# The first stage of an encoder kernel: c as one row, identity transposes ahead of the first product, and the second token half prepared in the gap at the loop's end

## The chip, the core and the metric

The kernel runs on one core of a Trainium2 chip. The core has a matrix engine (TensorE, PE in the rows), a vector engine (VectorE, DVE), an activation engine (ScalarE, ACT), a general engine (GpSimd, POOL) and SyncE (SP), which here issues all transfers between the chip's main memory and the on-chip memory. Each engine runs its own queue in order and waits on semaphores for what others produce. The metric is the device time of one execution, in microseconds (us); the median of the runs of the kernel before is 1440.84 us (three runs, 1440.55 to 1444.22).

## The reference

Two encoder layers over 1024 tokens of width 1024, one sequence, all in 32-bit floats. What matters here is how a layer begins:

```python
def _modulation(c, ada_w, ada_b):
    mod = jax.nn.silu(c) @ ada_w + ada_b
    shift, scale, gate = jnp.split(mod[:, None, :], 3, axis=-1)
    return shift, scale, gate

# layer i
shift, scale, gate = _modulation(c, ada_w[i], ada_b[i])
h = _rmsnorm(x, norm_g[i]) * (1.0 + scale) + shift
# layer 0 (differential attention)
proj = h @ w_in
q, k, v, z = jnp.split(proj, [DA_WIDTH, 2 * DA_WIDTH, 3 * DA_WIDTH], axis=-1)
q = _rope(q.reshape(b, s, 2 * DA_HEADS, DA_QK_DIM), positions)
```

So before any product of layer 0 there are the sums of squares of each token of x, the SiLU of c, and the products of c with 2048 columns of the modulation's weights (another 3072 columns are needed later).

## The kernel before, in words

**Precision.** Every product is made of three: both operands are split into a high part (rounded to the format that PE reads fast) and the rest, and high·high, high·rest and rest·high are added up in one accumulator (`mm3`, L181 to L183). A weight is split by a cast on ACT (L226, L544) and a subtraction on GpSimd or VectorE (L227, L545).

**The head.** c is loaded as a broadcast over all 128 partitions (L421, 512 KB), turned into 2·SiLU(c) by a tanh on ACT (L424) and one VectorE operation (L425), and copied into an accumulator bank of two bank widths (`cb`, L556), from which VectorE reads it. The four tiles of x's first token half (`xs0`, 128 tokens each) follow it in SP's queue. Their squares are summed on ACT (tiles 0 and 2, L531) and VectorE (tiles 1 and 3, L534); `inv_rms` (L463) and a power on GpSimd (L168) give the factors; ACT scales the first 256 columns (L564), VectorE the others (L618).

**The loop (first token half).** It runs over the 8 blocks `k` of 128 input features. For each, VectorE multiplies c with two tiles of modulation weights and sums (`mod_pair`: L431 twice, L439), which gives this block's shift and scale for each feature; PE turns four 128x128 pieces of x (`trh`, L485); ACT writes scale·x + shift as the high part `h0h` (L490) and in full as `h` (L492); GpSimd subtracts to get `h0l` (L495). One turn later PE adds the block into five accumulators: four of v (`vacc`, one for each 128 tokens, 512 columns; L635, L636 with `h0h`, L640 with `h0l`) and one of the K strip of head 0 (`kacc`, L637, L638, L641). Each turn needs two modulation tiles (`ada`, 512 KB each, 4 buffers), one tile of v's weights (`wvr`, 256 KB, 2 buffers) and half a tile of K weights.

**The gap.** After the loop stand: the squares of the second token half (`xs1`), the angles and sines of the rotary embedding (L572 to L591, with the table load that ACT needs for sines), the first half of head 0's q strip (`strip_half`, L181 to L183, 24 products of 128x512), the storing of the four v accumulators (`store_v`: cast L358, subtraction L359, transfer L361), the normalisation of `xs1` (L474).

**The second token half.** Eight blocks again: transposes (into `trh` and `trc` in turn), `h0h`, `h` and `h0l`, and 12 products a block, three blocks later. In between `mods_g` hands out the products of c for layer 1's modulation. Then come the K strip's second half, v's second 512 columns (`wv1`, accumulators `vps`), the q strip's second half, and the attention.

**What sets the order.** The program text is turned into one queue for each engine by a scheduler that goes by the order of the text and by when it expects an operand or a buffer to be ready. `tc.issue_after(i)` holds the instructions of its block behind `i` in their engine's queue; `tc.keep_in_program_order` keeps one where the text has it. A tile with a tag takes one of the `bufs` buffers of that tag in turn and waits until its last user is done.

## Time and profile before

| | |
|---|---|
| median of 3 runs | 1440.84 us |
| profiled execution | 1442.18 us, span of its instructions 1440.4 us |
| PE busy | 1390.9 us, 97% of the span |
| VectorE, ACT, GpSimd busy | 63%, 51%, 42% |
| mean granted clock of PE | 0.994 |
| first transpose of x on PE | at 14.35 us |
| longest wait of PE | 14.3 us, for the scaled x |
| DMA queue over the first 36 us | 325 GB/s |

A row of the timeline reads: start, duration, engine, line of the kernel, operation, what it writes and reads, shape, count, and in brackets how long the engine was idle just before it and for whom. PE's matmuls overlap, so the distance from one start to the next tells the pace, not the duration. The stretches (windows) give busy time and count of each engine between two moments, then the clock that the throttle granted to PE, the busy share of the transfer engines and their rate. A DMA's "us to landing" runs from its issue on SP until its data have arrived.

### The profile page before, as it was taken

How to read it: one execution, taken by the hardware profiler on the slowest of the kernel's cores; microseconds unless marked ns; L12 is line 12 of the kernel's file. 1: busy time of each engine (PE TensorE's matmuls, PEld its weight loads, DVE VectorE, ACT ScalarE, POOL GpSimd, SP SyncE). 2: the span in 40 equal slices, each digit the busy share in tenths (PEclk: the TensorE clock that was granted, in tenths of full speed). 3: DMA queues.
4: the chain of work that ended last, by engine and by line, in shares of the span. 5: the costliest groups of instructions: out<-in, count | busy, mean ns of one | idle time of the engine just before them, and what ended most of it. 6: DMA issues, size and time to landing. Idle time of an engine off the chain costs nothing. (4 is left out here: it accounts for less than half of the span.)

```text
span 1440.4 us, 20566 instructions
## 1 busy us (share of the span) xinstructions
PE 1390.9 (97%) x7388; PEld 1162.7 (81%) x7388; DVE 911.3 (63%) x1360; ACT 732.4 (51%) x1299; POOL 607.5 (42%) x483
## 2 busy tenths in 40 slices
PE   5999999999999999998999999989999999999997
PEld 4777788888888887887787787868888888888886
DVE  6657787667777767677445867254666555555355
ACT  5523366656565655566343643334554554545442
POOL 4316164656464646463561335313141331412562
PEclk9999999999999999999999999999999999999999
DMA  9777823333333333237653232566343433336663
GB/s 326 238 239 229 267 69 100 81 107 84 96 96 88 96 88 91 86 96 244 239 182 124 63 100 81 159 175 170 112 122 116 130 97 81 103 98 212 218 204 137
DMA packets 129766, 203.20 MB, mean 141 GB/s; under 512 B 18432, under 2 KB 55424, under 8 KB 129664
## 3 DMA queue, kind: packets, MB, share of 16 engines
q1 hardware_dynamic: 129664, 201.89, 46.4%
q8 instruction: 58, 0.95, 0.3%
q14 instruction: 44, 0.36, 0.1%
HBM read 132.68 MB, written 45.56 MB: 124 GB/s over the span
## 5 line engine op out<-in xcount | busy, mean ns | idle before, releaser
L381 ACT CAST pth<-tr 128x512 fp32r<-128x512 f32 x256 | 150.2, 587 | 277.3 <-PE tr L379 274.2
L396 DVE TENSOR_REDUCE nm<-s 128x1 f32<-128x1024 f32 x192 | 234.0, 1219 | 73.5 <-PE s L770 64.4
L382 DVE TENSOR_TENSOR ptl<-tr,pth 128x512 fp32r<-128x512 f32 x256 | 176.2, 688 | 137.5 <-ACT pth L381 136.8
L227 POOL TENSOR_TENSOR wl<-wraw,wh 128x512 fp32r<-128x512 f32 (+2 forms) x82 | 102.7, 1255 | 231.9 <-ACT wh L226 198.1
L398 ACT ACTIVATE e<-s,nm 128x1024 f32<-128x1024 f32 x128 | 143.5, 1121 | 30.4 <-DVE nm L396 29.9
L379 PE MATMUL tr<-ident,e 128*128 128x128 f32 x1024 | 154.9, 274 | 4.1 <-DVE ptl L382 3.7
L379 PEld LDWEIGHTS tr<-ident,e 128*128 128x128 f32 x1024 | 121.5, 141 | 45.2 <-DVE ptl L382 21.3
L181 PE MATMUL acc<-h0h,wh 128*128 128x512 f32 x360 | 150.1, 417 | 2.2 <-DVE v_hl L359 2.2
L181 PE MATMUL pv<-pth,vt 128*128 128x256 f32 x512 | 147.4, 288 | 0.0
L182 PE MATMUL pv<-ptl,vt 128*128 128x256 f32 x512 | 146.3, 286 | 0.0
L183 PE MATMUL pv<-pth,vt 128*128 128x256 f32 x512 | 144.8, 283 | 0.0
L183 PE MATMUL acc<-h0h,wl 128*128 128x512 f32 x360 | 142.3, 395 | 0.7 <-POOL wl L227 0.7
L182 PE MATMUL acc<-h0l,wh 128*128 128x512 f32 x360 | 141.6, 393 | 0.0
L1010 POOL TENSOR_TENSOR wol<-wor,woh 128x512 fp32r<-128x512 f32 x64 | 84.5, 1338 | 86.2 <-ACT woh L1009 81.1
L181 PEld LDWEIGHTS pv<-pth,vt 128*128 128x128 f32 x512 | 97.7, 191 | 3.1 <-ACT pth L381 0.4
L182 PEld LDWEIGHTS pv<-ptl,vt 128*128 128x128 f32 x512 | 97.8, 191 | 2.6
L183 PEld LDWEIGHTS pv<-pth,vt 128*128 128x128 f32 x512 | 97.9, 191 | 0.1
L328 POOL TENSOR_TENSOR rp_sw<-rp_sw,sinT 128x512 f32<-128x512 f32 x42 | 55.2, 1315 | 75.3 <-DMA rp_sw<-rp_raw 70.7
L770 PE MATMUL s<-ks,qa 128*128 128x512 f32 x256 | 82.2, 402 | 3.1 <-DVE e L778 2.7
L323 POOL TENSOR_TENSOR rp_r<-rp_raw,cosT 128x512 f32<-128x512 f32 x38 | 49.8, 1311 | 83.4 <-ACT rp_raw L318 52.3
L778 DVE SCALAR_TENSOR_TENSOR e<-s,z,e 128x1024 f32<-128x1024 f32 x64 | 82.1, 1283 | 2.1
L770 PE MATMUL s<-ks,qb 128*128 128x512 f32 x256 | 81.0, 395 | 0.0
(600 smaller groups left out, 3343.5 us busy)
## 6 DMA issues: line engine op xcount, KB each, us to landing
ada<-in_ada_ss SPq DMA_DIRECT2D x32, 512.0 KB, 6.1
wraw<-in_w_s SPq DMA_DIRECT2D x64, 256.0 KB, 2.9
vS<-v_hl SPq DMA_DIRECT2D x32, 512.0 KB, 5.2
vt<-vS SPq DMA_DIRECT2D x32, 512.0 KB, 4.0
wor<-in_w_out SPq DMA_DIRECT2D x64, 256.0 KB, 3.9
rp_sw<-rp_raw SPq DMA_DIRECT2D x168, 64.0 KB, 2.0
bc_s<-bc_d SPq DMA_DIRECT2D x34, 256.0 KB, 4.3
oS<-bc_s SPq DMA_DIRECT2D x30, 256.0 KB, 2.2
```

The costliest lines, as they stand in the source:

```text
L181: PE.matmul(psum, ah, bh, start=first, stop=False)
L182: PE.matmul(psum, ah, bl, start=False, stop=False)
L183: PE.matmul(psum, al, bh, start=False, stop=last)
L227: sub = (V if pair_of else G).tensor_sub(l_[:, :n], raw[:, :n], f32v(h_[:, :n]))
L379: PE.transpose(tr[:, j, :], p[:, kt * P : (kt + 1) * P], ident)
L381: mk["S"] = S.copy(pth[kh][:, :, dst], tr).ins
L382: mk["V"] = V.tensor_sub(ptl[kh][:, :, dst], tr, f32v(pth[kh][:, :, dst])).ins
L396: mk["V"] = V.reduce_max(nm, s_ps, axis=AX.X, negate=True).ins
L398: mk["S"] = S.activation(e, s_ps, AF.Exp, bias=nm, scale=1.0, accum_out=zs).ins
L770: PE.matmul(s_ps[:, kc * HF : (kc + 1) * HF], src[:, c, ql], KS[h][kc][:, c, :], start=fst, stop=not fst)
L778: combined.append(V.scalar_tensor_tensor(out=e0, in0=e1, scalar=z1[:, 0:1], in1=e0, op0=ALU.mult, op1=ALU.add).ins)
L1010: in_turn(G.tensor_sub(lo, raw, f32v(hi)))
```

## The change

- c is loaded as one row (4 KB). Its SiLU is computed on one partition and spread over the 128 partitions of `cb` by two products with a row of ones, full-precision 32-bit, 512 columns each. The copy that later modulations read is made from `cb` on ACT at block 2.
- PE gets 64 transposes of the identity ahead of the first transposes of x, the two products standing behind the seventeenth; 12 more stand between the first four transposes of x and the first product.
- The first token half's factors are computed for three tiles together and for the fourth alone, whose squares are shared by ACT and VectorE. Only the first 256 columns of x are scaled ahead of the loop; the rest follows in two pieces at blocks 0 to 2, on VectorE for tiles 0 and 1, on ACT for 2 and 3.
- `ada` has 6 buffers; the positions are loaded at block 2 instead of ahead of the loop; `h0l` is subtracted by GpSimd and VectorE in turn.
- In the loop the K strip's products run one block later than v's; the products of the first block's first two accumulators stand ahead of the second block's transposes (`v_high`, `pre`).
- The angles are computed at block 5; the table for sines is loaded right behind the last `h`; then come the q weights' splits (rest on GpSimd), the squares of `xs1`, and behind the first `store_v` the sines and the normalisation of `xs1`. The q strip is cut in two: five blocks, then the rest among the second half's first transposes.
- The second token half's last two blocks are added accumulator by accumulator. All its `h` are written by ACT.

Three places of the queues. First, PE's beginning, before (`trh` are pieces of x turned, `vacc` v's accumulators):

```order
L485 MATMUL trh<-ident,xt 128x128 x4
L635 MATMUL vacc<-wvh,h0h_0_102 128x512
L636 MATMUL vacc<-wvl,h0h_0_102 128x512
L635 MATMUL vacc<-wvh,h0h_0_102 128x512
L485 MATMUL trh<-ident,xt 128x128 x4
```

and now (`warm` is the bank that the identity transposes write):

```order
L575 MATMUL warm<-ident 128x128 x17
L435 MATMUL cb<-c_146,ones 128x512 x2
L575 MATMUL warm<-ident 128x128 x47
L494 MATMUL trh<-ident,xt 128x128 x4
L632 MATMUL vacc<-ident 128x128 x12
L646 MATMUL vacc<-wvh,h0h_0_102 128x512
```

78 instructions of PE are new, all of them here.

Second, PE at the q strip's end and the second token half's beginning (`acc` is the strip's accumulator, `xt` and `xth` are tiles of the second half), before:

```order
L183 MATMUL acc<-h0h_0_130,wq_455 128x512
L485 MATMUL trh<-ident,xt 128x128 x2
L485 MATMUL trh<-ident,xth 128x128 x2
L485 MATMUL trc<-ident,xt 128x128 x2
L485 MATMUL trc<-ident,xth 128x128 x2
L181 MATMUL vacc<-wvh,h0h_1_104 128x512
```

and now:

```order
L185 MATMUL acc<-h0h_0_122,wq_623 128x512
L494 MATMUL trh<-ident,xt 128x128
L186 MATMUL acc<-h0l_0_123,wq_623 128x512
L187 MATMUL acc<-h0h_0_122,wq_623 128x512
L494 MATMUL trh<-ident,xt 128x128
L494 MATMUL trh<-ident,xth 128x128
L185 MATMUL acc<-h0h_0_126,wq_623 128x512
L494 MATMUL trh<-ident,xth 128x128
```

The first four transposes moved from behind the strip's 24 products to behind its 16th, 18th and 19th.

Third, SP's queue from the stores of v (`vS`) to the weights of v's second 512 columns (`wvr`), before:

```order
L361 DMA vS_0_69<-v_hl 256x4x128 x2
L415 DMA ada<-in_ada_ss 128x1024 x2
L541 DMA wvr<-in_w_v 128x512 x2
L415 DMA ada<-in_ada_ss 128x1024 x2
L541 DMA wvr<-in_w_v 128x512 x2
L415 DMA ada<-in_ada_ss 128x1024
L361 DMA vS_0_69<-v_hl 256x4x128 x2
```

and now:

```order
L364 DMA vS_0_69<-v_hl 256x4x128 x2
L419 DMA ada<-in_ada_ss 128x1024 x6
L364 DMA vS_0_69<-v_hl 256x4x128 x2
L553 DMA wvr<-in_w_v 128x512 x2
L364 DMA vS_0_69<-v_hl 256x4x128 x2
L553 DMA wvr<-in_w_v 128x512 x2
L326 DMA rp_sw<-rp_raw 32x512 x3
L553 DMA wvr<-in_w_v 128x512 x2
```

Before, one `wvr` stands still further ahead, behind the tables' stores; now the first two stand behind the fifth and sixth store of v. From a few products behind the attention's first scores on, the queues of all engines hold the same instructions in the same order as before.

The diff, cut to its core (what is left out names instructions for `issue_after`, or passes an engine or a raw tile through a helper):

```diff
-ADA_B = 4
+ADA_B = 6
+WARM = 64
+WARM_H = 12
+WARM_C = 16
 X1_AT = 6
-WQ_AT = 6
+Q_CHUNK = 5
+ANG_AT = 5
...
-        sub = (V if pair_of else G).tensor_sub(l_[:, :n], raw[:, :n], f32v(h_[:, :n]))
+        sub = (lo_on or (V if pair_of else G)).tensor_sub(l_[:, :n], raw[:, :n], f32v(h_[:, :n]))
...
-    def load_c(pl, th, **kw):
-
-        c2 = pl.tile([P, D], F32, name="c2", **kw)
-        SP.dma_start(c2, A["c"].to_broadcast([P, D]))
-
-        def fin():
-            S.activation(th, c2, AF.Tanh, scale=0.5)
-            V.scalar_tensor_tensor(out=c2, in0=th, scalar=1.0, in1=c2, op0=ALU.add, op1=ALU.mult)
-
-        return c2, fin
+    def load_c(pl):
+        c1 = pl.tile([P, D], F32, name="c1", tag="xt", bufs=6)
+        SP.dma_start(c1[0:1, :], A["c"])
+        return c1
+
+    def spread_c(pl, c1):
+
+        th = pl.tile([P, D], F32, name="cth", tag="xt", bufs=6)
+        silu = [S.activation(th[0:1, :], c1[0:1, :], AF.Tanh, scale=0.5).ins]
+        silu.append(V.scalar_tensor_tensor(out=c1[0:1, :], in0=th[0:1, :], scalar=1.0, in1=c1[0:1, :], op0=ALU.add, op1=ALU.mult).ins)
+        cb = bank("cb", "cb", [P, D])
+        for f in range(2):
+            fs = slice(f * HF, f * HF + HF)
+            PE.matmul(cb[:, fs], ones[0:1, :], c1[0:1, fs], start=True, stop=True)
+        return cb, silu
...
-    th = p1.tile([P, D], F32, name="cth", tag="ada", bufs=ADA_B)
-    c2, c_fin = load_c(p1b, th)
-    xs0 = load_x(0)
-    posi = p1.tile([P, 256], I32, name="posi", tag="rot", bufs=3)
-    SP.dma_start(posi, A["pos"])
-    c_fin()
-    cb = bank("cb", "cb", [P, D])
-    S.copy(cb, c2)
-
     def ada0(j):
         return [mod_load(A["ada_ss0"][j, i], p1, ADA_B) for i in range(2)]
+    c1 = load_c(p1)
+    xs0 = load_x(0)
     wm0 = ada0(0)
-    y0 = inv_rms(sq_x(xs0, X_ACT0), 4)
+    warm = bank("tr", "warm", [P, 4, P])
+    for i in range(WARM):
+        PE.transpose(warm[:, i % 4, :], ident, ident)
+        if i == WARM_C:
+            cb, silu = spread_c(p1, c1)
+    c2 = p1b.tile([P, D], F32, name="c2")
+    y0 = [inv_rms(sq_x(xs0[:3], X_ACT0), 3)]
+    ss3 = [sm.tile([P, 1], F32, name=f"xs3{i}") for i in range(2)]
+    with tc.issue_after(silu[0]):
+        S.activation(p1.tile([P, D], BF16, name="junk", tag="junk", bufs=1)[:, :HF], xs0[3][0][:, :HF], AF.Square, accum_out=ss3[0])
+    junk3 = p1.tile([P, D], BF16, name="junk2", tag="h32", bufs=2)
+    with tc.issue_after(inv_rms.last):
+        V.tensor_tensor_reduce(out=junk3[:, HF:], in0=xs0[3][0][:, HF:], in1=xs0[3][0][:, HF:], scale=1.0, scalar=0.0, op0=ALU.mult, op1=ALU.add, accum_out=ss3[1])
+    V.tensor_add(ss3[1], ss3[1], ss3[0])
+    y0.append(inv_rms(ss3[1], 1))
+    y0 = [y0[0][:, j : j + 1] for j in range(3)] + [y0[1][:, 0:1]]
     for j in range(4):
-        S.mul(xs0[j][0][:, :X_CUT], xs0[j][0][:, :X_CUT], y0[:, j : j + 1])
+        S.mul(xs0[j][0][:, :X_CUT], xs0[j][0][:, :X_CUT], y0[j])
...
+    def idle_turns(n):
+        for i in range(n):
+            tc.keep_in_program_order(PE.transpose(vacc[3][:, (i % 4) * P : (i % 4 + 1) * P], ident, ident))
+
...
+    def v_high(k0, tts):
+        for tt in tts:
+            c_ = slice(tt * P, (tt + 1) * P)
+            PE.matmul(vacc[tt], h0[k0][0][0][:, c_], wv0[k0][0], start=k0 == 0, stop=False)
+            last = PE.matmul(vacc[tt], h0[k0][0][0][:, c_], wv0[k0][1], start=False, stop=False)
+        return last.ins
+
+    def split_wk(raw):
+        for d_, w_ in zip(wk0, split_strip(raw)):
+            d_ += w_
+
     for k in range(-1, KT + SKEW):
         if k + 1 < KT:
             wm = wm0 if k < 0 else ada0(k + 1)
-            wv0.append(load_wv(0, k + 1, 0, A["w_v0"][k + 1, 0]))
+            wv_raw = fetch_wv(A["w_v0"][k + 1, 0])
+            if k != 0:
+                wv0.append(split_wv(wv_raw))
             if k % 4 == 0:
-                for d_, w_ in zip(wk0, load_strip([A["w_s0"][1, 0, k // 4]], [4])):
-                    d_ += w_
-            m_last = mod_pair(0, k + 1, wm, cb)
-        if k < 0:
+                wk_raw = fetch_strip([A["w_s0"][1, 0, k // 4]], [4])
+                if k:
+                    split_wk(wk_raw)
+            with tc.issue_after(inv_rms.last) if k < 0 else nullcontext():
+                m_last = mod_pair(0, k + 1, wm, cb)
+        if k in (0, 1):
             with tc.issue_after(m_last):
-                for j in range(4):
-                    V.tensor_scalar(xs0[j][0][:, X_CUT:], xs0[j][0][:, X_CUT:], y0[:, j : j + 1], None, op0=ALU.mult)
-        if k == KT - 1:
-            with tc.issue_after(m_last):
-                angles()
+                for j in (0, 1):
+                    cs = slice(X_CUT + 256 * k, X_CUT + 256 if k == 0 else D)
+                    V.tensor_scalar(xs0[j][0][:, cs], xs0[j][0][:, cs], y0[j], None, op0=ALU.mult)
         if k == X1_AT:
+            wq_raw = fetch_strip([A["w_s0"][0, 0, f] for f in range(2)], [4, 4])
             xs1 = load_x(1)
-        if k == WQ_AT:
-            wq0 = load_strip([A["w_s0"][0, 0, f] for f in range(2)], [4, 4], None, ada_pair)
-            q_split = load_strip.last
+        if k == 2:
+            posi = p1.tile([P, 256], I32, name="posi", tag="rot", bufs=3)
+            SP.dma_start(posi, A["pos"])
+            S.copy(c2, cb)
+        pre = range(2) if k == 1 else ()
+        after = nullcontext()
+        if pre:
+            after = tc.issue_after(v_high(0, pre))
         if 0 <= k < KT:
-            h_chunk(0, xs0, k, h0[k][0], p1, act=True)
+            with after:
+                h0l_last = h_chunk(0, xs0, k, h0[k][0], p1, V if k % 2 else G, act=True)
+        if k == ANG_AT:
+            with tc.issue_after(h0l_last):
+                ang = angles()
+        if k == 0:
+            idle_turns(WARM_H)
+            with tc.issue_after(h_chunk.act):
+                wv0.append(split_wv(wv_raw))
+                split_wk(wk_raw)
+        if k in (1, 2):
+            with tc.issue_after(h_chunk.act):
+                for j in (2, 3):
+                    cs = slice(X_CUT + 256 * (k - 1), X_CUT + 256 if k == 1 else D)
+                    S.mul(xs0[j][0][:, cs], xs0[j][0][:, cs], y0[j])
         if k < SKEW:
             continue
-        k0, (wh, wl) = k - SKEW, wv0[k - SKEW]
-        hh, hl = h0[k0][0]
-        for tt in range(4):
-            c_ = slice(tt * P, (tt + 1) * P)
-            PE.matmul(vacc[tt], hh[:, c_], wh, start=k0 == 0, stop=False)
-            PE.matmul(vacc[tt], hh[:, c_], wl, start=False, stop=False)
-        PE.matmul(kacc, wk0[0][k0], hh, start=k0 == 0, stop=False)
-        PE.matmul(kacc, wk0[1][k0], hh, start=False, stop=False)
+        k0 = k - SKEW
+        hl, wh = h0[k0][0][1], wv0[k0][0]
+        v_high(k0, range(len(pre), 4))
+        if k0:
+            mm3(kacc, wk0[0][k0 - 1], wk0[1][k0 - 1], *h0[k0 - 1][0], k0 == 1, False)
         for tt in range(4):
             PE.matmul(vacc[tt], hl[:, tt * P : (tt + 1) * P], wh, start=False, stop=k0 == KT - 1)
-        PE.matmul(kacc, wk0[0][k0], hl, start=False, stop=k0 == KT - 1)
-    norm_x(sq_x(xs1), xs1)
-    load_tables()
-
-    qacc = strip_half(wq0, h0, 0)
+        if k0 == KT - 1:
+            mm3(kacc, wk0[0][k0], wk0[1][k0], *h0[k0][0], False, True)
+    with tc.issue_after(h_chunk.act):
+        S.activation(nil, nil, AF.Sin)
+        wq0 = split_strip(wq_raw, None, ada_pair, G)
+        ss1 = sm.tile([P, 4], F32, name="xss")
+        sq_x(xs1[:2], (0, 1), ss1)
+        sq_x(xs1[2:3], (0,), ss1[:, 2:3])
+    with tc.issue_after(h0l_last):
+        sq_x(xs1[3:], (), ss1[:, 3:4])
+    qgen = gen_half(wq0, h0, 0, lambda acc: QF.append(acc))
+    for k in range(Q_CHUNK):
+        next(qgen)
+    q_last = gen_half.last
     for tt in range(4):
-        store_v(0, p1b, vacc[tt], tt, 0)
+        a_, v_ = store_v(0, p1b, vacc[tt], tt, 0)
+        if tt == 0:
+            with tc.issue_after(a_), tc.issue_after(v_):
+                sines(*ang)
+                norm_x(ss1, xs1, (2,))
+                x1_last = norm_x.last
+            load_tables()
     vacc = [bank("acc", "vacc") for _ in range(4)]
     for k in range(KT + SKEW1):
+        if k == 1:
+            for _ in qgen:
+                pass
         if k < KT:
-            if k > 0:
-                next(mods_g)
-            with tc.issue_after(q_split):
-                h_last = h_chunk(0, xs1, k, h0[k][1], p1, V if k in HL_V else G, k % 2 == 1)
+            if k > 1:
+                with tc.issue_after(x1_last):
+                    for _ in range(2 if k == 5 else 1):
+                        next(mods_g)
+            with tc.issue_after(q_last):
+                h_last = h_chunk(0, xs1, k, h0[k][1], p1, V if k in HL_V else G, k % 2 == 1, act=True)
         if k >= SKEW1:
             k0 = k - SKEW1
             hh, hl = h0[k0][1]
             for tt in range(4):
-                c_ = slice(tt * P, (tt + 1) * P)
-                mm3(vacc[tt], hh[:, c_], hl[:, c_], wv0[k0][0], wv0[k0][1], k0 == 0, k0 == KT - 1)
+                for k1 in () if k0 == KT - 2 else range(k0 - 1, k0 + 1) if k0 == KT - 1 else (k0,):
+                    hh, hl = h0[k1][1]
+                    c_ = slice(tt * P, (tt + 1) * P)
+                    mm3(vacc[tt], hh[:, c_], hl[:, c_], wv0[k1][0], wv0[k1][1], k1 == 0, k1 == KT - 1)
...
-    q_done(0)(qacc, 0)
+    q_done(0)(QF[0], 0)
```

51 lines of the change are left out of this document (31 added, 20 removed).

## The prediction

> **What bounds the kernel now.** I read the page's busy times first, then the timeline of TensorE (PE) and of the others over the first 115 us, and last the stretches cut at the clock's steps.
>
> ```profile
> PE 1390.9 (97%) x7388; PEld 1162.7 (81%) x7388; DVE 911.3 (63%) x1360; ACT 732.4 (51%) x1299; POOL 607.5 (42%) x483
> ```
>
> PE is busy 97% of the span, so a change pays only where PE stands still or runs slowly.
>
> The timeline of PE gives four marks: the first product at 16.89, the loop's last at 52.67 (ends 53.07), the first of the second token half at 63.80, that half's last at 88.78. In the brackets stands how long PE was idle before a row, and for whom; these waits and the slow stretches are what the first stage has to give.
>
> ```profile
> 14.35 1.67 PE L485 MATMUL trh<-ident,xt 128*128 128x128 f32 x4 [14.35 <-ACT xt L564]
> 16.89 0.80 PE L635 MATMUL vacc<-wvh,h0h 128*128 128x512 f32 x1 [0.87 <-ACT h0h L490]
> ...
> 18.79 1.06 PE L485 MATMUL trh<-ident,xt 128*128 128x128 f32 x4
> 19.50 0.78 PE L636 MATMUL vacc<-wvl,h0h 128*128 128x512 f32 x1
> ...
> 20.50 0.63 PE L636 MATMUL vacc<-wvl,h0h 128*128 128x512 f32 x1
> 20.92 0.63 PE L635 MATMUL vacc<-wvh,h0h 128*128 128x512 f32 x1
> ...
> 24.38 0.60 PE L485 MATMUL trh<-ident,xt 128*128 128x128 f32 x4
> ...
> 43.85 0.60 PE L485 MATMUL trh<-ident,xt 128*128 128x128 f32 x4
> ...
> 51.64 1.19 PE L640 MATMUL vacc<-wvh,h0l 128*128 128x512 f32 x4 [2.16 <-POOL h0l L495]
> 52.67 0.40 PE L641 MATMUL kacc<-h0l,wh 128*128 128x512 f32 x1
> 53.94 0.80 PE L181 MATMUL acc<-h0h,wq 128*128 128x512 f32 x1 [0.87 <-ACT wq L226]
> ...
> 62.33 0.38 PE L485 MATMUL trh<-ident,xt 128*128 128x128 f32 x2
> ...
> 63.80 0.50 PE L181 MATMUL vacc<-wvh,h0h 128*128 128x512 f32 x1 [0.43 <-ACT h0h L490]
> ...
> 88.78 0.39 PE L183 MATMUL vacc<-wvh,h0l 128*128 128x512 f32 x1
> 90.12 0.50 PE L181 MATMUL acc<-h0h,wh 128*128 128x512 f32 x1 [0.94 <-DVE v_hl L359]
> ```
>
> At 20.5 products start 0.42 us apart, in the q strip from 53.94 too; elsewhere 0.23. The stretches below are cut at the clock's steps (us, PE busy, granted clock, DMA share, GB/s): each is 3.41 us, the grain in which the clock moves here.
>
> ```profile
> 15.59:19.00 3.41, 2.46 (x7) 1.00 1.04 400
> 19.00:22.42 3.42, 3.42 (x11) 1.00 0.78 250
> ...
> 49.73:53.14 3.41, 1.43 (x5) 1.00 0.50 137
> 53.14:56.55 3.41, 2.61 (x6) 0.50 0.92 259
> 56.55:59.97 3.42, 3.42 (x9) 0.50 1.14 274
> ...
> 674.40:677.80 3.40, 1.71 (x10) 1.00 0.46 164
> ```
>
> A stretch 42% busy (1.43 of 3.41) dropped the clock to half, one 50% busy did not, one 76% busy did not bring it back, a full one did. Before 22.42 no granted clock is on record (it reads 1.00), but the spacing says half.
>
> **The start.** c (512 KB, broadcast) is replaced by one row, so x no longer queues behind it. The rows of the old chain:
>
> ```profile
> 2.50 0.15 DVE L159 TENSOR_SCALAR g<-vec 128x1 f32<-128x1 f32 x1 [1.51 <-DMA vec<-in_vec]
> 5.82 1.06 ACT L424 ACTIVATE cth<-c 128x1024 f32<-128x1024 f32 x1 [3.82 <-DMA c<-in_c]
> 6.91 1.23 DVE L425 SCALAR_TENSOR_TENSOR c<-cth,c 128x1024 f32<-128x1024 f32 x1 [4.25 <-ACT cth L424]
> 15.36 0.16 DVE L439 SCALAR_TENSOR_TENSOR moda<-moda,vec 128x1 f32<-128x1 f32 x1
> L827 PE MATMUL rb<-dg,ones x8: 273/275/276, 1353.8 to 1354.6; 128*128 128x128 f32 x8
> ```
>
> vec, issued just ahead of c, lands at 2.5, so c's row lands near 3.0; tanh 1.06 and the multiply 1.23 make it ready at 5.4 (the operations cost per element of the row, not per partition). What queued behind the broadcast moves up by at least its bytes (1.3 us at 400 GB/s) and at most the 3.3 between vec and c; I take 2.3, which brings scaled x from 14.35 to 12.0 and the first scale from 15.5 to 13.2. By then PE itself is the later one. Its queue: 17 identity transposes (from 1.4, at the slow 0.18 us of the group at 18.79), then two products that spread c. They are not in this trace; the nearest, rb, writes four full-precision products of 128 columns as eight records 0.11 us apart, so two of 512 columns are four records of 0.45: 1.8 us at full clock, 3.6 at half. From 5.4 that ends at 9.0. PE is now busy without a gap, so by the stretches the clock steps up between 8.8 and 12.2, say 10.5. The other 47 transposes: 8 slow ones to 10.5, 39 at 0.11 (eight from 62.33 in 0.86) to 14.8. Four real transposes (0.43) and 12 idle ones (1.3) lead to a **first product at 16.5**, 15.8 to 17.2 with the step: hardly earlier (0.4), but at full speed.
>
> **The loop.** From 24.38 to 43.85 five turns take 19.47, 3.89 each, so eight without the first group of transposes take 30.7. Between 53.07 and 16.89 lie 36.2; the difference is the slow start (2.8) and the 2.16 before L640:
>
> ```profile
> 38.06 1.30 POOL L227 TENSOR_TENSOR wl<-wraw,wh 128x512 fp32r<-128x512 f32 x1 [0.96 <-ACT wh L226]
> ...
> 47.55 1.28 ACT L585 ACT_TABLE_LOAD   x1
> ...
> 49.48 0.76 ACT L492 ACTIVATE h<-trh,modb,moda 128x512 f32<-128x512 f32 x1
> 50.31 1.27 POOL L495 TENSOR_TENSOR h0l<-h,h0h 128x512 fp32r<-128x512 f32 x1 [4.70 <-ACT h L492]
> ```
>
> Two squares, a table load and two sines stood ahead of the last h activation on ScalarE (ACT), and GpSimd waited 4.7 for it. The change puts them behind it. I add 0.2: the scaling of x's second 256 columns waits on ACT behind the third wv tile, whose load is issued only when GpSimd's first split frees a buffer. If that load comes 1 us later, all of it shows. The loop needs 1.3 MB a turn; the queue gave 400 GB/s while it was fed (15.59 to 19.00), 3.3 us a turn, and six ada buffers instead of four let it run ahead. **Saved 5.3**; loop end near 47.4.
>
> **The gap at the loop's end.** From 53.07 to 63.80 are 10.7: 0.9 wait, 24 products of which the first 14 ran at half clock, 8 transposes, 0.4 wait. The q weights' high and low parts (0.61 on ACT, 1.30 on GpSimd for such a tile) now come out while the last 33 products (7.6 us) run, so the strip should follow at once. But x's second half must be normalised beneath it:
>
> ```profile
> 52.17 0.59 ACT L358 CAST v_hl<-vacc 128x512 fp32r<-128x512 f32 x1 [1.02 <-PE vacc L640]
> 52.65 0.63 ACT L531 ACTIVATE junk<-xth 128x512 bf16<-128x512 f32 x1
> 52.79 0.69 DVE L359 TENSOR_TENSOR v_hl<-vacc,v_hl 128x512 fp32r<-128x512 f32 x1 [2.74 <-ACT v_hl L358]
> 56.59 1.01 POOL L168 TENSOR_TENSOR rq_y<-xss,mhalf 128x4 f32<-128x4 f32 x1 [5.01 <-DVE xss L463]
> 57.64 1.42 DVE L474 TENSOR_SCALAR xt<-xt,rq_y 128x1024 f32<-128x1024 f32 x2 [1.12 <-POOL rq_y L168]
> ```
>
> In the new order ACT runs, from 1.1 before the loop's end, v_hl, two half squares with their reads (0.7 each), a sine (0.3) and v_hl again: 2.9. Then on VectorE the second subtraction 0.7 and the scalar step 0.2, GpSimd 1.0, and 0.7 for the first tile of x: ready 4.4 after the loop's end, the last one 5.7. PE meets the first of these transposes after 16 strip products (3.7) and stands behind it, about 0.8, then 0.4 for the others; five products and eight transposes follow. First product 8.0 after the loop's end, where 6.8 would be bare work: **saved 2.7**. That much idle leaves a stretch over 60% busy, so the clock should hold; if not, it costs 1.7.
>
> **The second half and after.** It keeps its 25.4 us. Its last two contraction steps go accumulator by accumulator, so the bank wait of 0.94 behind v_hl goes. In exchange SyncE (SP) now issues the weights of v's second column half behind the stores of v; before, the first was issued at 51.47.
>
> ```profile
> DMA to landing us min/median/max: 4.5/5.1/5.3
> DMA to landing us min/median/max: 2.8/5.6/8.9
> wraw<-in_w_s SPq DMA_DIRECT2D x64, 256.0 KB, 2.9
> 89.20:115.00 25.80, 23.47 (x98) 18.19 (x99) 14.77 (x24) 6.78 (x13) 6.27 (x5) 1.00 0.88 258
> ```
>
> (wvr's landing between 75 and 110 us; the same in the first 60 us; the page's median for strips of that size; and a stretch whose first busy time is PE's.) Two raw buffers make four pairs in a chain of landing L plus 1.6 for the splits; PE needs the fourth pair 81 products, 18.6 us, after the half's end, and the chain, begun 0.3 before it, delivers its first high part (0.6) at 4L + 5.1, so it stalls 4L - 13.5: none at 2.9, 6.9 at 5.1. Before, this stretch held 25.8 - 23.5 = 2.3 of stalls, the 0.94 among them. With the ada loads already done by then the queue is lighter; I take L = 4, a stall of 2.5, **net nothing**, with bounds of +2.3 and -4.6.
>
> From the attention's first scores on, near 156 us, the order of all engines is the same in both kernels, and PE is nearly without waits there, so the gain is carried to the end.
>
> **Sum.** 0.4 + 5.3 + 2.7 = 8.4 us. The profiled span is 1440.4 (1442.18 with what lies around it); the median of the runs is 1440.84, so 1440.84 - 8.4 = **1432.4 us**. Its own range, from the clock's step, the strip's stall and L, is 1428 to 1437.
>
> **Rivals.**
> *Transposes do not release the clock.* Speaking for it: no stretch of this trace is full of transposes alone. Against: the stretch at 674.4, with few products and four transposes, kept it. Then the 47 take 8.5 to 9.4 and the last 16 another 2.9; the first product comes at 20.9, 4.0 later than now, and as slow for as long. Of the gains there remain the 2.2 before L640, 0.3 of pace and 2.7 in the gap: 2.2 + 0.3 + 2.7 - 4.0 = 1.2, **1439.6**.
> [...]
> *Late v weights*, the other side: at L = 6.05 the stall eats the 2.3 and all 8.4; at L = 7.5 it is 16.5, and 16.5 - 2.3 - 8.4 = 5.8 is lost: **1446.6**. For it: transfers took up to 8.9 in the first 60 us. Against: none over 5.3 between 75 and 110, with 88% of the DMA time taken.
>
> **Numbers.** Forecast 0.71, clock 0.20, late weights 0.09. A change under 0.3% (4.3 us, so 1436.5 to 1445.2) can hardly be told from none. Of the forecast's cases nine in ten lie below 1436.5, and of the clock's one in ten, since some of the products in the warm-up may count: faster 0.64 + 0.02 = 0.66. Within: 0.07 + 0.16 + 0.02 = 0.25. Slower: 0.02 + 0.07 = 0.09. The range takes in the clock's case and leaves out the late weights and the best of all bounds: 1428 to 1441.
>
> **What would show it.** PE spacing of 0.23 from the first product, which stands near 16.5; no wait before L706 of the last turn; the strip following the loop at once at granted clock 1.00, with a wait of about 1 us at a transpose of xt; PE waits on wvh or wvl of some 2.5 us after the K strip. Transposes at 0.18 to the end of the first queue, a first product after 20, or wv waits over 5 us would make it wrong.

## The result, and the profile after

The change makes the kernel slower. The median is 1455.99 us (four runs, 1453.69 to 1457.56), where the kernel before, run beside it, has 1442.47: a ratio of 1.0093 with a 95% interval of 1.0070 to 1.0115. The profiled execution takes 1456.66 us with a span of 1454.9, where before it was 1442.18 and 1440.4. The forecast of 1432.4 is missed by 24 us and on the wrong side; the time lies outside the range and beyond every rival.

I put the same marks on both traces, and beside them what the prediction's steps give (its sum carried on from mark to mark):

| mark (us from the span's start) | before | by the prediction | after |
|---|---|---|---|
| first product | 16.89 | 16.5 | 18.88 |
| end of the loop | 53.06 | 47.4 | 52.37 |
| first product of the second token half | 63.80 | 55.4 | 63.24 |
| first product of v's second columns (`vps`) | 95.69 | 87.3 | 93.61 |
| attention's first scores | 155.72 | 147.3 | 167.60 |
| end of the span | 1440.4 | 1432.0 | 1454.9 |

So two things went wrong. The first stage gives 0.6 instead of 8.4 us: 2.0 lost at the first product, 2.7 gained in the loop, 0.1 lost in the gap, where the sum had gains of 0.4, 5.3 and 2.7. And 14 us are lost in a stretch that the change hardly touches, between the first `vps` product and the first scores. The stretches between the marks, in the profile's windows, first of the kernel before and then of the changed kernel (length, then busy time of PE, PE's weight loads, VectorE, ACT, GpSimd, each with its count; granted clock, DMA share, GB/s):

```profile
16.89:63.80 46.91, 43.36 (x181) 34.33 (x181) 32.72 (x61) 26.40 (x47) 24.17 (x19) 0.93 0.92 309
63.80:95.69 31.89, 30.95 (x145) 24.91 (x145) 21.25 (x32) 10.32 (x16) 7.63 (x6) 1.00 0.60 188
95.69:155.72 60.03, 58.61 (x255) 47.30 (x254) 39.12 (x55) 17.37 (x30) 25.28 (x16) 1.00 0.83 257
```

```profile
18.88:63.24 44.36, 40.39 (x187) 31.57 (x186) 33.79 (x63) 30.08 (x53) 20.91 (x16) 0.96 0.80 272
63.24:93.61 30.37, 29.92 (x143) 24.30 (x141) 12.45 (x20) 12.97 (x21) 8.04 (x6) 1.00 0.72 213
93.61:167.60 73.99, 64.65 (x259) 51.51 (x260) 41.01 (x58) 18.92 (x32) 23.86 (x16) 0.93 0.74 230
```

Read the third row of each. It grew by 13.96 us: PE's idle time from 1.4 to 9.3 (7.9), and its busy time by 6.0 with hardly more products. The second part is the clock, 0.93 instead of 1.00: three of its 3.41 us stretches ran at half. Two of them:

```profile
154.07:157.48 3.41, 2.54 (x6) 2.05 (x7) 3.25 (x6) 0.10 (x1) 0.00 (x0) 0.50 1.07 367
157.48:160.89 3.41, 3.41 (x9) 2.64 (x9) 1.91 (x5) 0.58 (x1) 0.00 (x0) 0.50 0.96 285
```

About half of the busy time in a stretch at half clock is lost (products start 0.43 us apart there, 0.23 at full clock, as from 161.00 on), here 3.0 us, and 1.7 in a third one that starts at 113.11; the remaining 1.4 is six `vps` products more that stand ahead of the scores in the new order (187 instead of 181).

The waits of PE from 90 to 168 us, changed kernel (in all, times, longest):

```profile
PE vps L185 <- DVE v_hl L362: 6.0, 1, 6.0
PE vps L186 <- DVE wvl L563: 2.0, 2, 1.0
PE acc L185 <- ACT rp_raw L324: 1.4, 1, 1.4
PE vps L185 <- ACT wvh L562: 0.5, 1, 0.5
```

The waits for weights are there (2.5, and 1.4 for `rp_raw`), but the largest is one for a bank: a `vps` accumulator can't be begun because ACT and VectorE haven't copied the previous contents out (`v_hl`). It follows from one late cast. First the changed kernel's timeline on ACT, GpSimd, SP and PE, then the same instructions of the kernel before:

```profile
125.23 0.39 PE L187 MATMUL vps<-wvh,h0l 128*128 128x512 f32 x1
125.71 0.59 ACT L362 CAST v_hl<-vps 128x512 fp32r<-128x512 f32 x1 [8.43 <-PE vps L187]
126.20 0.62 ACT L344 CAST ks<-rp_r 64x512 fp32r<-64x512 f32 x1
...
127.31 1.29 POOL L346 TENSOR_TENSOR ks<-rp_r,ks 64x512 fp32r<-64x512 f32 x1 [9.55 <-ACT ks L344]
...
135.97 4.79 SPq L209 DMA_DIRECT2D wraw<-in_w_s  x2
...
146.94 0.63 SPq L364 DMA_DIRECT2D vS<-v_hl  x1
...
153.58 0.58 ACT L362 CAST v_hl<-vps 128x512 fp32r<-128x512 f32 x1 [17.63 <-DMA vS<-v_hl]
154.94 0.80 PE L185 MATMUL vps<-wvh,h0h 128*128 128x512 f32 x1 [5.98 <-DVE v_hl L362]
167.60 0.62 PE L858 MATMUL s<-ks,qa 128*128 128x512 f32 x2
```

```profile
108.42 0.39 PE L183 MATMUL vps<-wvh,h0l 128*128 128x512 f32 x1
109.18 0.59 ACT L358 CAST v_hl<-vps 128x512 fp32r<-128x512 f32 x1
115.46 0.61 ACT L340 CAST ks<-rp_r 64x512 fp32r<-64x512 f32 x1
...
116.19 2.15 POOL L342 TENSOR_TENSOR ks<-rp_r,ks 64x512 fp32r<-64x512 f32 x1
...
128.63 3.86 SPq L205 DMA_DIRECT2D wraw<-in_w_s  x2
...
138.68 0.63 SPq L361 DMA_DIRECT2D vS<-v_hl  x1
...
145.12 0.59 ACT L358 CAST v_hl<-vps 128x512 fp32r<-128x512 f32 x1 [13.32 <-DMA vS<-v_hl]
```

Before, PE finished the first tile of v's second columns at 108.8, and ACT's cast of it was out of the way when the keys (`ks`) were ready. Now the last weights of that tile come behind other work, PE finishes it at 125.6 behind a strip, and ACT, whose queue runs in order, stands 8.43 us at the cast with the key casts behind it. GpSimd waits 9.55 for a key cast, SP's next strip load (`wraw`), which waits for a split on GpSimd behind the keys, goes out 7.3 later, the store `vS` behind it 8.3 later, the buffer of `v_hl` that this store frees comes 8.5 later (153.58), and with it PE's bank. All of that is one chain, 7 to 11 us late at each link.

### The profile page after: what moved, and what is told of

Its sections match the earlier page's. It is cut to its first block, busy times and chain, and to the rows that moved or that the text cites. A ratio compares the mean times of both kernels' runs of the same rounds, so it can differ in the third digit from the quotient of the medians.

```text
span 1454.9 us, 20732 instructions
## 1 busy us (share of the span) xinstructions
PE 1408.0 (97%) x7468; PEld 1174.5 (81%) x7468; DVE 907.9 (62%) x1358; ACT 740.8 (51%) x1312; POOL 604.5 (42%) x483
```

## The experiments

The kernel before was run beside each group of experiments, so the ratio to it is what is compared; its medians were 1441.88, 1442.83 and 1442.73 us. One hundredth of a per cent is 0.14 us. Times within a run are those of its one profiled execution.

**The v weights issued early.** The first two pairs of the weights of v's second columns go ahead of the stores of the second token half, as one stood before:

```diff
+    wv1 = [load_wv(A["w_v0"][k, 1], V) for k in range(2)]
     for tt in range(4):
         store_v(0, p1b, vacc[tt], 4 + tt, 0)
...
-    wv1 = [load_wv(A["w_v0"][k, 1], V) for k in range(KT)]
+    wv1 += [load_wv(A["w_v0"][k, 1], V) for k in range(2, KT)]
```

> The changed kernel, with the first two loads of v's second-column weights put ahead of the stores of v's second token half in the program; SyncE then issues the first pair ahead of the last four stores of v's first columns, the four tiles' products come in another order and the first of those tiles is complete before the last z strip instead of behind it. Theory A (late weights set off a chain: the cast of the first tile stands ahead of the key casts on ScalarE, GpSimd's key splits wait behind it, the stores of v are issued late and TensorE waits 6.0 us for a bank, with half a clock behind it): waits for weights fall from 3.8 to under 1.5 us, the 6.0 us wait goes, the time falls by 9 to 14 us, to 1442 to 1447. Theory B (the stores and modulation loads of this stretch are simply too many for the queue in the new order): waits move, the time stays within 3 us of 1456.

Measured: 1446.14 us, ratio 1.0027 (1.0014 to 1.0040), so two thirds of the loss are gone. The `vps` cast stands at 115.64 with the key casts right behind it, and the first scores at 156.38.

**The cast behind the keys.** The weights stay late; only the first tile's cast is held behind the key casts in ACT's queue:

```diff
-            S.copy(t[64:128, 1, :], r[64:128])
+            stack_k.last = S.copy(t[64:128, 1, :], r[64:128]).ins
...
-            store_v(0, p1b, acc, tt, fh)
+            with tc.issue_after(stack_k.last) if tt == 0 else nullcontext():
+                store_v(0, p1b, acc, tt, fh)
```

> The changed kernel, with one thing moved: the cast of the first tile of v's second columns goes behind the four key casts on ScalarE (its store so goes a few places back on SyncE); TensorE's order is untouched and the weights come as late as before. Theory A: the wait of 9.55 us of GpSimd for the key cast goes, the q copies leave near 133 instead of 140.8, TensorE's 6.0 us wait for a bank falls to under 1.5 and the clock stays full there: 8 to 11 us less, 1445 to 1448, with the waits for weights (0.45, 0.97, 1.03, 1.35) unchanged. Theory B (bank wait is owed to late weights or to the stores alone): the wait moves to another store and the time stays within 3 us of 1456.

Measured: 1447.11 us, ratio 1.0040 (1.0025 to 1.0055). PE's waits for weights are those of the changed kernel (2.1 for `wvl`), and yet the chain is back where it was before:

```profile
116.01 1.80 POOL L346 TENSOR_TENSOR ks<-rp_r,ks 64x512 fp32r<-64x512 f32 x1
...
126.75 3.28 SPq L209 DMA_DIRECT2D wraw<-in_w_s  x2
...
155.87 0.62 PE L859 MATMUL s<-ks,qa 128*128 128x512 f32 x2
```

In this execution the first `vps` product stands at 90.61, 3.0 earlier than in the changed kernel, because the clock happened to step up early (at 4.7 instead of 14.1, last section); the other 8.7 of the 11.7 us gained at the scores lie in the stretch of the cast. By the ratios the edit takes away 0.53 of the 0.93%; 0.40% are left. This settles the main cause: not the wait of PE for the weights, but the place of one cast in ACT's queue.

**The cast ahead of the squares.** At the loop's end the cast and subtraction of the first accumulator go ahead of the squares of the second token half, so that the strip finds its bank free:

```diff
+    first_v = store_v(0, p1b, vacc[0], 0, 0)
+    with tc.issue_after(first_v[0]):
...
-    with tc.issue_after(h0l_last):
+    with tc.issue_after(first_v[1]):
...
-        a_, v_ = store_v(0, p1b, vacc[tt], tt, 0)
+        a_, v_ = first_v if tt == 0 else store_v(0, p1b, vacc[tt], tt, 0)
```

> The changed kernel, with the first cast of v (which frees the q strip's bank) put ahead of the squares of x's second half on ScalarE, and the squares behind it. Theory A (the gap is set by x's statistics, and the bank wait only stands in front of the same wait): the 2.23 us before the strip falls under 0.5, about 1.5 to 2.5 us appear ahead of the transposes of x instead, the half clock at 55 goes, the first product of the second half comes at 62 to 63.3 instead of 63.24, and the time falls by 0 to 1.5 us. Theory B (the bank wait and its half clock are the whole loss of the gap): the first product at 59.5 to 60.5, 2.7 to 3.7 us less.

Measured: 1453.74 us, ratio 1.0088 (1.0074 to 1.0101). The wait at the strip is gone, the clock stays full (products 0.23 apart from 51.93 on), and the second token half begins 8.55 after the loop's end (51.55) instead of 10.87:

```profile
51.59 0.50 PE L185 MATMUL acc<-h0h,wq 128*128 128x512 f32 x1
...
60.10 0.50 PE L185 MATMUL vacc<-wvh,h0h 128*128 128x512 f32 x1 [0.76 <-ACT h0h L499]
```

That mark came out at the more favourable of the expected values, though 0.8 of the 3.1 us gained were there at the loop's end already. But the time doesn't follow: the ratio can't be told from the change's own (0.05% less), the cast of `vps` still waits 8.34 for PE, and the bank wait is 6.0 as it was. At the first scores (163.87) the gain is 3.7.

**A shorter warm-up.** 36 identity transposes instead of 64:

```diff
-WARM = 64
+WARM = 36
```

> The changed kernel with 36 instead of 64 identity transposes ahead of the first real one. Theory A (the first product waits for the queue of transposes, x being scaled at 12.5): the first product comes at 14.5 to 15.2 instead of 18.88, at full spacing 0.23 at once or after one step of the clock; of the 4 us at most half is left at the loop's end, since the modulation loads pace the loop, so the loop ends 1 to 3 us earlier (49.5 to 51.5) and the time falls by 0 to 3 us. Theory B (the products would come at half clock): spacing of 0.43 over at least 10 products, loop end unchanged.

Measured: 1447.95 us, ratio 1.0045 (1.0029 to 1.0061): more than any expectation (0.48% less, where at most 3 us were expected). The first product comes at 14.33, the loop ends at 49.79, the scores at 159.35. Of the 8.3 gained at the scores, 4.6 are there at the first `vps` product already (88.97), 1.7 are the half-clock stretch at 113, which isn't there, and 1.3 are shorter waits for weights and `rp_raw` (2.5 instead of 3.8); the bank wait is one longer, 7.0. The rest wasn't taken apart. The earlier product shows another limit at once: the loop's end now waits 1.93 for `h0h`.

**All four together.**

> The changed kernel with the four edits of the earlier runs together: weights early, first cast of v's second columns behind the key casts, first cast of v ahead of the squares, 36 warm-up transposes. Theory C (the first scores are set by a second chain: SyncE's weight strips that wait for GpSimd, the q copies, the modulation loads and the stores of v behind them, with 95% of the DMA time taken from 140 to 170): TensorE reaches the tiles of v's second columns 6 to 8 us earlier than before the change, but the first scores start at 153 to 156.5 (155.72 before), a wait of 3 us or more for a bank stands there, and the time is 1438 to 1443. Theory D (the single gains add up): first scores at 148 to 151, time 1432 to 1436.

Measured: 1443.07 us, ratio 1.0005 (0.9995 to 1.0015). By the ratios the four by themselves take away 0.66, 0.53, 0.05 and 0.48%, 25 us; together they take away 0.88%, 12.7 us. The first `vps` product is at 89.15, 6.5 earlier than in the kernel before, and the first scores at 156.25, no earlier. Of the 6.5, 1.4 are again the six products more; the rest stands in PE's waits and on ACT:

```profile
PE vps L185 <- DVE v_hl L362: 3.5, 1, 3.5
```

```profile
127.27 0.59 ACT L362 CAST v_hl<-vps 128x512 fp32r<-128x512 f32 x1
136.37 0.59 ACT L362 CAST v_hl<-vps 128x512 fp32r<-128x512 f32 x1 [8.51 <-DMA vS<-v_hl]
143.39 0.58 ACT L362 CAST v_hl<-vps 128x512 fp32r<-128x512 f32 x1 [6.43 <-DMA vS<-v_hl]
```

ACT can't cast the next `vps` tile because both buffers of `v_hl` are still being stored. PE's wait of 3.5 for a bank is followed by a stretch at half clock (products 0.43 apart from 146.1 to 149.1), which costs about 1.7. In the kernel before ACT waited for a store as well (13.32 at 145.12, above), but PE had work meanwhile; with PE earlier, this second chain decides. From here the question was what paces it.

**Modulation rows spread out.** In that stretch VectorE forms products for layer 1's modulation, and ACT's waits also name them (`gcol`). Seven of these rows are handed out earlier, in the second token half and in the K and Q strips, once on the repaired change and once on the kernel before:

```diff
-MODS = (2, 2, 2, 2, 3, 2, 0, 0)
+MODS = (1, 1, 1, 1, 1, 1, 0, 0)
...
-                    for _ in range(2 if k == 5 else 1):
+                    for _ in range(2 if k > 3 else 1):
...
-        if i % 4 == 3:
+        if i % 2 == 1:
```

> As the run with all four edits, and seven of the thirteen modulation rows that were loaded during the tiles of v's second columns are taken earlier (three in the second half's loop, four in the K and Q strips). Theory C: with less in the chain the first scores start 4 us or more earlier than in that run, at 147 to 151, the bank wait falls under 1.5 us, and the time falls by 4 to 7 us against it, below the kernel before (1433 to 1438). Theory D: the rows are not what holds the first scores; under 2 us of difference.

> The kernel before the change, with the same seven modulation rows taken earlier (three in the second half's loop, four in the K and Q strips); nothing of the change. Theory C: TensorE had no idle time from 115 to 156 there, so lighter modulations alone bring the first scores forward by at most 2 us: 1438 to 1443. Theory D': the chain alone held the kernel before, and the time falls by 4 us or more.

Measured: 1451.06 (1.0059; 1.0047 to 1.0071) and 1447.85 (1.0035; 1.0023 to 1.0048). Both are slower than what they start from, against the expectations. In the first the weights of v now queue behind the rows' loads (a wait of 4.5 for `wvh`), and the bank wait grows to 6.7; in the second the first `vps` cast moves from 109.2 to 115.0 and the bank wait to 5.7. PE's waits from 85 to 165 us in the first of the two:

```profile
PE vps L185 <- DVE v_hl L362: 7.3, 2, 6.7
PE vps L185 <- ACT wvh L562: 4.5, 1, 4.5
```

So handing out the rows earlier didn't shorten the chain here, and it delayed the weights.

**Three rows only.** `MODS = (2, 1, 2, 1, 2, 2, 0, 0)`, the loop's line as above, nothing in the strips:

> As the run with all four edits, with only the three rows of the second half's loop taken earlier. Theory C: three of thirteen rows, some 1.3 us of DVE and 1.7 us of transfer each, bring the first scores forward by 2 to 4 us against that run: 1435 to 1440. Theory D: under 1.5 us of difference.

Measured: 1442.94, ratio 1.0005 (0.9997 to 1.0014), the same as without. Again PE waits 4.6 for the first weights, so that the bank wait falls to 1.7 and the scores come at 155.68 all the same: here it made no difference whether PE waited early or late.

**A third store buffer.** The repaired change with three buffers for `v_hl` in layer 0:

```diff
-VB = (2, 5)
+VB = (3, 5)
```

> As the run with all four edits, with three instead of two buffers for the stores of v (nothing else; the four stores of the second half then stand together on SyncE). Theory C2 (with two buffers each cast of v waits until the store of the tile two before has landed, some 6.5 us after its issue, so the chain from the q copies through stores and casts ends at 155 to 156 whatever TensorE does): the bank wait of 3.5 us ahead of the first scores falls under 1 us, the first scores start at 150 to 154 and the time falls by 2 to 5 us, to 1438 to 1441. Rival (the modulation dots between the subtractions on VectorE hold it): first scores within 1 us of 156.2, time 1442 to 1444.

Measured: 1438.35 us (1435.87 to 1440.97), ratio 0.9967 (0.9955 to 0.9979): by the ratios 0.38%, 5.5 us, faster than without the buffer, and the only kernel more than 0.3% below the one before, though its interval reaches to 0.21%. PE no longer waits for a bank ahead of the scores, and they come ten microseconds earlier:

```profile
145.44 0.62 PE L862 MATMUL s<-ks,qa 128*128 128x512 f32 x2
...
155.67 1.07 PE L862 MATMUL s<-ks,qa 128*128 128x512 f32 x2 [2.27 <-DVE e L870]
```

Not all of these ten are gain: 170 `vps` products instead of 187 stand ahead of the first scores, the others behind them, and a wait for VectorE's `e` (2.27) is new, with half clock behind it (granted clock 0.50 from 155.80 to 166.00).

**The first weights earlier still.** The first pair ahead of the second token half's loop, three rows earlier as above; then the same with three buffers; and the buffer on the kernel before alone:

> As the run with three modulation rows earlier, with the first pair of v's second-column weights asked for ahead of the second half's loop. Theory C2: the wait of 4.6 us for the first weights goes, TensorE reaches the tiles of v's second columns at 88.5 to 90 instead of 92, but stands longer for a bank (3 to 6 us): first scores at 154 to 156, time 1440 to 1444. Theory D (what TensorE saves arrives): first scores at 150 to 152, time 1436 to 1439.

> As the run before it in this list (weights earlier, three modulation rows earlier, all four edits), with three buffers for the stores of v. Theory C2: no bank wait over 1 us ahead of the first scores, which start at 148 to 153; time 1434 to 1440, below the kernel before. Rival: first scores still at 154 to 156, time 1440 to 1444.

> The kernel before, with three buffers for the stores of v and nothing else. Theory C2: TensorE was the bound there as well (no idle time from 115 to 156), so the first scores move by at most 1.5 us and the time stays within 2 us of 1442. Rival: the buffers alone bring 3 us or more.

Measured: 1441.46 (0.9989; 0.9981 to 0.9998), 1440.43 (0.9979; 0.9971 to 0.9988) and 1445.01 (1.0017; 1.0005 to 1.0030). Without the buffer the earlier weights bring `vps` to 87.45, and the bank takes 4.5 back (at 93.45). With it, the time is 0.10% lower, which the intervals don't tell from nothing, just outside what was expected, and not better than with the simpler repairs. On the kernel before, the buffer brings no time (the interval lies just above 1; within 2 us of 1442 was expected). But there too the first scores moved by 6.2 us, where 1.5 at most were expected:

```profile
149.50 0.62 PE L770 MATMUL s<-ks,qa 128*128 128x512 f32 x2
...
171.63 0.62 PE L770 MATMUL s<-ks,qa 128*128 128x512 f32 x2
```

The second row is the seventeenth product of the scores. Ahead of it PE has as many products with the buffer as without, ahead of the first it hasn't:

| kernel | first scores | seventeenth | median |
|---|---|---|---|
| before | 155.72 | 170.78 | 1442.73 |
| before, third buffer | 149.50 | 171.63 | 1445.01 |
| all four | 156.25 | 172.47 | 1443.07 |
| all four, third buffer | 145.44 | 169.88 | 1438.35 |

So most of the earlier first scores is products put behind them: on the repaired change 2.6 of the 10.8 us are left at the seventeenth, on the kernel before nothing. In these runs the buffer is worth something only together with the gain of the first stage, and there clearly in one of two pairs.

## Why the prediction was wrong

**The stretch from the first `vps` product to the first scores, taken over unchanged.** This is the step that failed most. But for the wait for weights, which was put at net nothing, the sum holds no term for it, and its 60.0 us became 74.0: 7.9 of idle PE, 4.7 of half clock and 1.4 of six products more. (What the prediction says of the time from the scores on, that the gain is carried to the end, held for the loss within 2.6 us.) In the kernel before, PE has hardly a wait in this stretch (1.4 idle in 60.0) and is busy all the time from 115 to 140 us:

```profile
115.00:140.00 25.00, 25.00 (x112) 20.73 (x111) 18.87 (x23) 10.08 (x17) 19.01 (x12) 1.00 0.68 212
```

I took that for room to move. But the buffers and stores stood just behind PE: a gain of 6.5 at the first `vps` product (all four repairs) became none at the scores. That the buffers are part of this second bound is shown by the third one on the repaired change: the bank wait went, and the time fell by 5.5 us; with the earlier weights it fell by 1.4, no more than the noise. What paces the chain beside them, the landing of a store (a median of 6.3 us for the `vS` stores from 100 to 160 us before) or the place of its issue in SP's queue, no run separates.

**"The second half and after: net nothing".** The term was to be a stall of PE of 2.5 against 2.3; measured are 1.5 less to the first `vps` product and then 14.0 more. The waits of PE for these weights are 2.5 (0.5 + 2.0), and the loads landed after 4.1 (median), where 4 was taken, so the term, as it was defined, was right. But it priced the late weights only by PE. What stood behind them in ACT's queue wasn't named, although the prediction had the same pattern before its eyes at the loop's end, where GpSimd waits for ACT. The rival of late weights had the place right and the mechanism wrong: it needed L above 6, and the time came from the cast.

**The start.** Right were x's scaling (12.54, predicted 12.0), the first scale (13.40, predicted 13.2), and the two products with ones (3.77, predicted 3.6; 1.98 at full clock in the run with the cast behind the keys, where products of split parts of the same 512 columns start 0.23 apart). One row took as long as 128, as the prediction has it: 1.06 for the tanh and 1.21 for the multiply of c's row, 1.06 and 1.23 before. Wrong was the moment of the clock's step: 14.12 instead of 10.5. That is partly chance: in two other runs of the same code it came before 6 (4.7 and about 5.5, last section).

```profile
5.71 3.77 PE L435 MATMUL cb<-c,ones 1*128 1x512 f32 x4 [0.48 <-DVE c L431]
9.42 7.62 PE L575 MATMUL warm<-ident 128*128 128x128 f32 x47
17.15 0.67 PE L494 MATMUL trh<-ident,xt 128*128 128x128 f32 x4
18.88 0.48 PE L646 MATMUL vacc<-wvh,h0h 128*128 128x512 f32 x1
```

The transposes stand 0.21 us apart until 14.1 and 0.11 from then on; the stretch from 7.30 to 10.71 was full (3.41 of 3.41 busy), mostly with products of one row, and didn't raise it. So some 21 slow transposes rather than 8 (0.21 apart, where 0.18 was taken), a first product 2.4 later than forecast and 2.0 later than before. The rival by which transposes don't release the clock is refuted all the same. The clearest record is in the run with the cast behind the keys, whose start is the same code; the windows of that run, cut at the clock's steps:

```profile
4.69:8.11 3.42, 3.35 (x17) 1.86 (x16) 1.60 (x3) 1.47 (x3) 0.00 (x0) 1.00 1.03 410
8.11:11.52 3.41, 3.41 (x19) 3.41 (x17) 2.20 (x6) 2.57 (x7) 1.78 (x2) 0.50 1.02 410
11.52:14.93 3.41, 3.31 (x30) 3.08 (x29) 2.94 (x8) 1.36 (x4) 1.28 (x1) 1.00 1.03 402
```

The middle stretch holds identity transposes alone at half clock (0.50, 3.41 of 3.41 busy), and after it the granted clock is full (1.00). The first one was 98% busy, 2.0 us of it with the two one-row products, and was followed by a drop.

**The loop.** The turn was right (3.88, predicted from 3.89), the eight turns weren't: 33.5 us from the first product to the end instead of 30.9. The angles, which stood behind the loop, now stand in VectorE's queue ahead of the last scale; ACT and PE wait for that:

```profile
44.03 1.39 DVE L608 SCALAR_TENSOR_TENSOR ang<-kk,ang 128x256 f32<-128x256 f32 x1
46.88 0.14 DVE L448 SCALAR_TENSOR_TENSOR moda<-moda,vec 128x1 f32<-128x1 f32 x1
...
47.12 0.78 ACT L499 ACTIVATE h0h<-trh,modb,moda 128x512 fp32r<-128x512 f32 x1 [4.15 <-DVE moda L448]
47.95 0.50 PE L646 MATMUL vacc<-wvh,h0h 128*128 128x512 f32 x1 [1.05 <-ACT h0h L499]
```

The stall that the prediction saw leave (2.16 behind GpSimd's `h0l`) moved to VectorE; that the angles run at block 5 was in the change, and their cost on VectorE, 2.7 us (42.69 to 45.34), was not in the sum. Two of them took 1.31 and 1.39 us while GpSimd was subtracting; two like the second took 0.41 and 0.43 when it was idle. Of the 2.6 us that the turns are over the forecast, PE's waits are 1.6 (1.05 here, 0.56 at 31.15).

Nor is an early start kept by itself. In the run with the early weights the first product stands at 14.43, 4.5 earlier than in the changed kernel, and the loop ends at 51.25, only 1.1 earlier: the pieces of x that are scaled in the loop come too late (waits of 0.45 and 1.90), and half clock follows (products 0.43 apart from 23.08 to 25.64). The 1.90 is the case that the prediction saw and put at 0.2, ACT's scaling behind the third tile of v's weights, for whose load ACT waits 2.45.

**The gap.** 10.87 us instead of 8.0. "The strip should follow at once" was wrong: its accumulator is a bank that `v_hl` must first free, and that cast stands behind two squares on ACT.

```profile
51.02 1.05 ACT L542 ACTIVATE junk<-xt 128x1024 bf16<-128x1024 f32 x1
...
53.25 0.56 ACT L362 CAST v_hl<-vacc 128x512 fp32r<-128x512 f32 x1
...
54.59 0.50 PE L185 MATMUL acc<-h0h,wq 128*128 128x512 f32 x1 [2.23 <-DVE v_hl L362]
```

The 2.23 us were then followed by a stretch at half clock (granted clock 0.50 from 55.08 to 58.49). With the cast ahead, the gap was 8.55, near the forecast, and its waits at the transposes and the first `h0h` 0.67 and 0.76 (predicted 0.8 and 0.4): the rest of this step was right.

**What stays open.** From the first scores to the end the changed kernel takes 1287.3 us in its profiled execution and the kernel before 1284.7. Of these 2.6 more, 1.2 lie in the 50 us behind the scores (a bank wait of 1.7 and one more stretch at half clock, 0.50 from 174.55 to 177.96); the other 1.4 have no cause that I could find, and single executions of kernels with the same order there differ by more: 1290.1 with the early weights, 1283.5 with the shorter warm-up. So it isn't explained either why the early weights, with scores at 156.38, still stand at 1.0027.

## What to carry to other kernels

An engine that is 97% busy without a wait can have a second chain right behind it: before a gain is carried on, look for when its banks, buffers and stores come free, and ask what happens if it arrives earlier. When an instruction's input gets later, what counts is less who waits for it than what stands behind the waiting instruction in its in-order queue; moving that one cast was worth nearly as much as giving it its input early (0.53 and 0.66%). And what is moved off the end of a loop lands ahead of something else: follow it on the engine that takes it. Two kernels can be compared at a mark only if the same work stands ahead of it: the first scores came ten microseconds earlier with most of that not gained.

## What the runs showed of the hardware

The first product stands at 18.88, 18.08, 15.91 and 14.43 us in four kernels whose code is the same up to there (the change, the cast ahead of the squares, the cast behind the keys, the early weights). By the spacing of PE's rows (transposes 0.21 us apart at half clock, 0.11 at full; the one-row products 3.77 and 3.78 in the first two kernels, 1.98 and 2.13 in the others), the clock first stepped up at 14.1, about 13.0, 4.7 and about 5.5. Within a trace its steps are 3.41 us or a multiple of that apart (in the changed kernel up at 14.12, down at 55.08, up at 58.49, down at 154.07, up at 160.89), but the first steps of the four lie some 1.1, 8.6 and 9.4 us from that of the changed kernel, which are no multiples: the stretches lie differently against the program's start in each. So here the step moved by over 9 us and the first product by 4.5 with the same code. The fast starts of some experiments are thus partly luck, and part of what the shorter warm-up gained may be too; its single trace doesn't tell.

Two stretches were full or nearly full, mostly with products that have one row of weights, and the clock didn't rise after the one and fell after the other. In the changed kernel these products kept PE busy for 2.1 of the 3.41 us from 7.30 to 10.71, identity transposes for the rest; in the run with the cast behind the keys for 2.0 of the 3.42 us after which the clock fell at 8.11. My reading of the two is that such products hardly count as work for the clock: if they count as idle, the second stretch was 40% busy (1.35 of 3.42), and the prediction's rows had 42% as a stretch that dropped the clock. It is argued from these stretches alone; no run was made for it.

Long waits of PE were paid twice in the changed kernel: the 2.23 at the strip and the 5.98 at the bank were each followed by half clock (granted clock 0.50 for 3.41 and 6.82 us), by the spacing about 1.7 and 3.0 us more.
